# Seven products of quadrant sums for 14 of 22 feed-forward tiles, the last product in thirds, and the gate from one table

## The chip, the core and the metric

One core of a Trainium2 chip runs the whole program. The metric is the device time of one execution in microseconds (us), lower being better. Three runs of the kernel before took 2994.84, 2996.77 and 2997.41 us; the median is 2996.77.

## The reference, cut to what matters

The model is a chain of ten stages on 512 tokens of 1024 features in float32: two hybrid attention layers, then twice (feed-forward, HGRN2 and pooling mixer, memory cross-attention, feed-forward), and a last norm. The change lives in the four feed-forward stages (D_FF = 2816):

```python
def swiglu(h, w1, w3, w2):
    return (jax.nn.silu(h @ w1) * (h @ w3)) @ w2

x = x + 0.5 * swiglu(rmsnorm(x, ffn1_norm[l]), ffn1_w1[l], ffn1_w3[l], ffn1_w2[l])
```

## The kernel before, in words

Activations stand feature-major: features on the 128 partitions, the 512 tokens along the free axis, so x is eight tiles x0 to x7 of 128x512. Every dense product runs on the tensor engine (PE) in three passes: an operand is split exactly into a leading part (hi) and the rest (lo), and `mm3` (lines 296 to 298) issues hi*hi, hi*lo and lo*hi for each block of 128 features:

```python
self.nc.tensor.matmul(ps, ah, bh, start=first and i == 0, stop=False)   # L296
self.nc.tensor.matmul(ps, ah, bl, start=False, stop=False)              # L297
self.nc.tensor.matmul(ps, al, bh, start=False, stop=last and i == n - 1)  # L298
```

Each matmul has its own weight load (LDWEIGHTS, shown as PEld). Weights come from HBM through the SP queue in pieces `wraw` of up to 128x1024 (L270, four buffers); `chunk` (L287, L288) lets the scalar engine (ACT) write `whi` by a copy that rounds and the vector engine (DVE) write `wlo` by a subtraction. `whi` and `wlo` have two buffers each, so that the next chunk of weights is prepared while the present one is used.

A feed-forward stage (`ffn`) goes in two halves of 11 tiles. A tile is 128 columns of w1 and the same 128 columns of w3, each a unit of eight blocks, 24 matmuls of 512 columns, into one PSUM bank `mm` of three. The evacuation `ev` runs two units later. After the w1 unit, DVE multiplies the bank by `rt`, the tokens' 1/rms (L886, into `si`); silu is made of an exponential, a logarithm and an exponential on ACT (L504 to L506) between a clamp (L501) and two multiplications (L888, L889) on POOL (GpSimd). After the w3 unit DVE multiplies the bank by the gate (L893), ACT rounds the result into `hh` and DVE subtracts for `hl` (L256, L257). The w2 product of the half follows: eight units of 11 blocks (33 matmuls), each added to its x tile by one DVE operation (L901). So a stage has 22 x 48 + 8 x 66 = 1584 matmuls of 512 columns. In the second half the x tiles are at once split for the next stage (`ready`, L262, L263).

The order of the work on each engine is set by the order in which the program issues it, by the delays of `later` and `tick` (steps run so many units later), and by the tile framework's scheduler, which may move ready instructions ahead. On the chip each engine then runs its own list in order.

Of the kernel before, what the change touches and what calls it, by code (L numbers as in the profile page):

```python
# [29 lines left out]
NH = DFF // P // 2  # L30
# [6 lines left out]
# tiles of a tag get their room in program order, so work that runs at its own pace has a tag of its own  # L37
SLOTS = {"slot": 34, "alt": 12, "far": 11}
# [10 lines left out]
        "ffn1": "ql sb si",  # L49
        "mix": "hO ha1 ham hd he hk msh qh ql",  # L50
        "xa": "ql xq",
        "ffn2": "ql sb si",
# [3 lines left out]
# engines of the steps that more than one can take: V(ector), P(ool), A(ctivation)  # L56
# [42 lines left out]
def _const_layout():  # L99
    c = Cols()  # L100
    for name, w in (("ones", 128), ("eps", 1), ("bd", 128), ("ident", 128), ("dil", 512),
                    ("causal", 512), ("tri", 512), ("reset", 512), ("diag", 32), ("pool", 64)):
        c.add(name, w)
    return c
# [3 lines left out]
CONST_EARLY = CONST.at["dil"][0]  # L108


def _constants():
# [21 lines left out]
    # pairs s, t of 32 tokens in the two halves of a segment of 2 hs tokens  # L133
# [11 lines left out]
def _pack(i):  # L145
# [5 lines left out]
    # 8 frequencies x 16 blocks of 32 tokens  # L151
# [37 lines left out]
    for n in ("ffn1", "ffn2"):  # L189
        w1, w3, w2 = f(f"{n}_w1_2"), f(f"{n}_w3_2"), f(f"{n}_w2_2")  # L190
        A[f"{n}_w13"] = per(lambda l: np.concatenate([_chunks(w1[l], 128), _chunks(w3[l], 128)], 3))
        half = NH * P
        A[f"{n}_w2"] = per(lambda l: np.stack([_chunks(w2[l][h * half:(h + 1) * half], 128) for h in range(2)]))
# [13 lines left out]
# ---------------------------------------------------------------- the program  # L207
class Prog:
# [9 lines left out]
    # tiles  # L218
# [26 lines left out]
    def cst(self, name):  # L245
        o, w = CONST.at[name]
        return self.c[:, o:o + w]
# [5 lines left out]
    # exact split of float32 into two float32r parts  # L253
# [12 lines left out]
    def raw(self, flat, pieces=1):  # L266
# [4 lines left out]
        return t  # L271

    def chunk(self, ap, kt, c):
        """One chunk of a weight: both parts, [128, kt, c]."""
        nc = self.nc
        early, self.early = self.early, None
        hi = self._new(self.sb, [P, 2080], R, "whi", 2, "whi")
        lo = self._new(self.sb, [P, 2080], R, "wlo", 2, "wlo")
        n = kt * c
        flat = ap.rearrange("p k c -> p (k c)")  # L280
        step = -(-kt // 2) * c
        for o in range(0, n, step):
            e = min(o + step, n)
            raw = early[o // step] if early else self.raw(flat[:, o:e])
            for a in range(o, e, step // 2 if early else step):
                b = a + step // 2 if early else e
                nc.scalar.activation(hi[:, a:b], raw[:, a - o:b - o], AF.Copy)  # L287
                nc.vector.tensor_tensor(lo[:, a:b], raw[:, a - o:b - o], hi.bitcast(F32)[:, a:b], op=ALU.subtract)  # L288
        v = lambda t: t[:, :n].rearrange("p (k c) -> p k c", k=kt)
# [1095 lines left out]
```

## Time and profile before

| what | value |
|---|---|
| median of three runs | 2996.77 us |
| profiled execution: span from first to last instruction | 2992.6 us |
| its own time beside the span | not listed apart; the span lies 4.2 us below the runs' median |
| PE busy | 2929.1 us, 98% |
| DVE, ACT, POOL busy | 1674.1, 1406.6, 745.2 us |
| mean granted PE clock | 0.994 |

The span is what the profile divides among engines and lines; what the launch adds lies outside it. PE's busy time counts overlapping matmuls once. A matmul's own duration (0.39 us at 512 columns) is longer than the distance to the next one's start, because matmuls overlap in the pipeline; the distance from start to start is what a matmul costs in a row of them.

### The profile page before, as it was taken

What the parts mean: (1) busy time and instruction counts of PE and PEld (TensorE: products, weight loads), DVE (VectorE), ACT (ScalarE), POOL (GpSimd) and SP (SyncE); (2) the same over time, 40 slices, a digit from 0 to 9 for tenths busy, and PEclk for the clock granted to TensorE, in tenths of its full rate; (3) what the DMA queues carried; (4) which work ended last, traced back from release to release, by engine and by line L of the source; (5) the groups of instructions that cost most, each with busy time, mean ns of one, the idle gap of its engine ahead of it and who ended that gap; (6) DMA issues with size and microseconds to landing.
All of it is one profiled execution on the core that took longest, in us unless ns stands there. A gap on an engine that the chain in (4) does not pass through costs nothing.

```text
span 2992.6 us, 39832 instructions
## 1 busy us (share of the span) xinstructions
PE 2929.1 (98%) x15544; PEld 2372.5 (79%) x15544; DVE 1674.1 (56%) x2698; ACT 1406.6 (47%) x2334; POOL 745.2 (25%) x613
## 2 busy tenths in 40 slices
PE   7999999999999999999999999999999999999997
PEld 6777877778788887798888888888888798888886
DVE  7976678766533337785643333433347976643333
ACT  5876467664532434464443233432434654443342
POOL 3101131011331323331032132321323330132231
PEclk9999999999999999999999999999999999999999
DMA  4432233322223232243132323223232242232322
GB/s 159 121 103 82 95 113 94 106 80 94 96 80 107 87 96 89 68 131 99 57 99 79 111 90 99 97 76 111 83 107 83 79 134 85 71 98 79 110 75 76
DMA packets 93436, 284.10 MB, mean 95 GB/s; under 512 B 12656, under 2 KB 13056, under 8 KB 93120
## 3 DMA queue, kind: packets, MB, share of 16 engines
q1 hardware_dynamic: 92928, 281.26, 29.5%
q8 instruction: 122, 2.00, 0.3%
q14 instruction: 66, 0.54, 0.1%
q10 hardware_dynamic: 288, 0.28, 0.0%
q0 software_dynamic: 32, 0.02, 0.0%
HBM read 261.46 MB, written 2.10 MB: 88 GB/s over the span
## 4 chain that ended last, share of the span: by engine, by line
PE 86%; DVE 7%; ACT 2%; issue 1%; POOL 0%; DMA 0%; DVEq 0%; ACTq 0%; POOLq 0%
PE mm L296 27%; PE mm L297 26%; PE mm L298 26%; PE po L712 2%; DVE wlo L288 1%; PE pt L701 1%; PE aux L687 1%; PE aux L421 1%; PE aux L688 1%; PE po L1103 0%; PE aux L296 0%; PE aux L298 0%; PE aux L297 0%; ACT whi L287 0%; DVE hw L1020 0%
## 5 line engine op out<-in xcount | busy, mean ns | idle before, releaser
L296 PE MATMUL mm<-xsh,whi 128*128 128x512 f32 x2304 | 926.9, 403 | 16.9 <-DVE pol L263 8.1
L297 PE MATMUL mm<-xsl,whi 128*128 128x512 f32 x2304 | 910.5, 395 | 8.0 <-DVE xsl L263 7.6
L298 PE MATMUL mm<-xsh,wlo 128*128 128x512 f32 x2304 | 911.2, 396 | 0.0
L287 ACT ACTIVATE whi<-wraw 128x1024 fp32r<-128x1024 f32 (+4 forms) x526 | 498.5, 984 | 572.2 <-PE mm L297 408.0
L288 DVE TENSOR_TENSOR wlo<-wraw,whi 128x1024 fp32r<-128x1024 f32 (+4 forms) x526 | 596.5, 1165 | 110.4 <-ACT whi L287 106.2
L296 PEld LDWEIGHTS mm<-xsh,whi 128*128 128x128 f32 x2304 | 435.6, 189 | 128.4 <-issue 13.1
L297 PEld LDWEIGHTS mm<-xsl,whi 128*128 128x128 f32 x2304 | 435.7, 189 | 108.2 <-DVE xsl L263 14.5
L298 PEld LDWEIGHTS mm<-xsh,wlo 128*128 128x128 f32 x2304 | 435.1, 189 | 101.4 <-DVE wlo L288 0.2
L501 POOL TENSOR_SCALAR sb<-si 128x512 f32<-128x512 f32 x88 | 130.8, 1487 | 770.0 <-DVE si L886 770.0
L433 POOL TENSOR_TENSOR sq<-sq,sq 128x512 f32<-128x512 f32 (+1 forms) x97 | 132.0, 1361 | 722.5 <-ACT sq L430 711.0
L893 DVE TENSOR_TENSOR sb<-mm,sb 128x512 f32<-128x512 f32 x88 | 60.9, 692 | 435.2 <-POOL sb L889 435.2
L297 PE MATMUL mm<-hl,whi 128*128 128x512 f32 x704 | 277.4, 394 | 0.0
L296 PE MATMUL mm<-hh,whi 128*128 128x512 f32 x704 | 277.2, 394 | 0.0
L298 PE MATMUL mm<-hh,wlo 128*128 128x512 f32 x704 | 276.7, 393 | 0.0
L504 ACT ACTIVATE sb<-sb 128x512 f32<-128x512 f32 x88 | 55.8, 634 | 464.1 <-POOL sb L501 464.1
L901 DVE SCALAR_TENSOR_TENSOR x<-mm,x 128x512 f32<-128x512 f32 x64 | 44.3, 692 | 306.7 <-PE mm L298 306.7
L297 PEld LDWEIGHTS mm<-hl,whi 128*128 128x128 f32 x704 | 132.3, 188 | 30.8
L296 PEld LDWEIGHTS mm<-hh,whi 128*128 128x128 f32 x704 | 131.8, 187 | 31.3
L298 PEld LDWEIGHTS mm<-hh,wlo 128*128 128x128 f32 x704 | 132.5, 188 | 30.3
L886 DVE TENSOR_TENSOR si<-mm,rt 128x512 f32<-128x512 f32 x88 | 60.9, 692 | 134.4 <-PE mm L298 134.2
L889 POOL TENSOR_TENSOR sb<-sb,si 128x512 f32<-128x512 f32 x88 | 113.9, 1296 | 67.3 <-ACT sb L506 67.3
L888 POOL TENSOR_TENSOR si<-si,rt 128x512 f32<-128x512 f32 x88 | 114.9, 1306 | 7.3
(360 smaller groups left out, 4580.8 us busy)
## 6 DMA issues: line engine op xcount, KB each, us to landing
wraw<-in_ffn_w_dram SPq DMA_DIRECT2D x176, 512.0 KB
wraw<-in_ffn_w_dram SPq DMA_DIRECT2D x64, 384.0 KB
wraw<-in_ffn_w_dram SPq DMA_DIRECT2D x64, 320.0 KB
z<-z SPq DMA_DIRECT2D x128, 128.0 KB
wraw<-in_w_out_dram SPq DMA_DIRECT2D x32, 512.0 KB
wraw<-in_w_qk_dram SPq DMA_DIRECT2D x30, 512.0 KB
wraw<-in_w_g_dram SPq DMA_DIRECT2D x16, 512.0 KB
wraw<-in_w_gate_dram SPq DMA_DIRECT2D x16, 512.0 KB
```

Of the source, the lines that this page charges most:

```text
L287: nc.scalar.activation(hi[:, a:b], raw[:, a - o:b - o], AF.Copy)
L288: nc.vector.tensor_tensor(lo[:, a:b], raw[:, a - o:b - o], hi.bitcast(F32)[:, a:b], op=ALU.subtract)
L296: self.nc.tensor.matmul(ps, ah, bh, start=first and i == 0, stop=False)
L297: self.nc.tensor.matmul(ps, ah, bl, start=False, stop=False)
L298: self.nc.tensor.matmul(ps, al, bh, start=False, stop=last and i == n - 1)
L433: (eng or self.on("acc")).tensor_tensor(acc[:, :n], acc[:, :n], sq[:, :n], op=ALU.add)
L501: clamp.tensor_scalar(t, x, -40.0, None, op0=ALU.max)
L712: nc.tensor.matmul(self.po[rows, j * P:], v[j][:, 64 * h:64 * h + 64], ptS[b][:, o:o + T - j * P], start=j == 0, stop=j == 2)
L886: nc.vector.tensor_tensor(s, ps, r["r"], op=ALU.mult)
L888: nc.gpsimd.tensor_tensor(s, s, r["r"], op=ALU.mult)
L889: nc.gpsimd.tensor_tensor(b, b, s, op=ALU.mult)
L893: nc.vector.tensor_tensor(b, ps, b, op=ALU.mult)
```

## The change

In each feed-forward stage, 14 of the 22 tiles are computed another way. Take for one tile the matrix A of two rows (128 columns of w1; the same of w3) by two columns (the even-numbered 128-feature blocks of x; the odd-numbered), and B of two rows (even and odd blocks of x) by two columns (tokens 0 to 255, tokens 256 to 511). A B has four quadrants. Instead of eight quadrant products, seven products of sums of quadrants are made (Winograd's form of Strassen's method), each over four feature blocks and 256 tokens: 12 matmuls of 256 columns, 84 in all for the tile instead of 48 of 512 columns. The sums of the weights' quadrants (`sums`, L962) are made on DVE for each tile and then split into hi and lo as the raw weights are; the sums of x's quadrants (`seven_operands`, L906 to L909) are made once for a stage, during the first two tiles. The products' banks are put together by additions on DVE (L962 again, into a tile `early`). `PLAIN` says which tiles remain as they were ("1"), now in the order w1, w3 of `gated_pair`.

```diff
-NH = DFF // P // 2
+THIRDS = (8, 7, 7)
+PLAIN = ("11100100", "0010010", "0010010")
...
-        A[f"{n}_w13"] = per(lambda l: np.concatenate([_chunks(w1[l], 128), _chunks(w3[l], 128)], 3))
+        A[f"{n}_w13"] = per(lambda l: np.stack([_chunks(w[l], 128)[:, :, o::2] for w, o in ((w1, 0), (w1, 1), (w3, 1), (w3, 0))], 2))
...
+    def half(self, n):
+        return [self._new(self.sb, [P, 1040], R, "w", 8, "w" + e)[:, :n] for e in "hl"]
...
+    def seven(self, flat, mv, r, done):
...
+        def p0():
+            st["e"], st["o"] = (self.raw(flat[:, o:o + 1024]) for o in (0, 1024))
+            st["a"] = self.half(1024)
+            self.parted(st["a"], st["e"])
+        def p1():
+            f, e, o = wide("sums", 2), st["e"], st["o"]
+            st["f"] = f
+            add(f[:, :512], o[:, 512:], o[:, :512])
+            add(f[:, 512:], f[:, :512], e[:, :512])
+            st["s"] = self.half(1024)
+            self.parted(st["s"], f)
+        def p2():
+            g, e, o = wide("sums", 2), st["e"], st["o"]
+            add(g[:, :512], e[:, :512], o[:, 512:])
+            add(g[:, 512:], st["f"][:, 512:], e[:, 512:])
+            st["t"] = self.half(1024)
+            self.parted(st["t"], g)
+        def p3():
+            st["d"] = self.half(512)
+            self.parted(st["d"], st["o"][:, :512])
...
+        def m4():
+            product("y2", 1, "d", 0, "t4")
+            q, g = st["q"], self.s(nm="sb")
+            self.later(2, lambda: add(q[:, H:3 * H], st["y2"], st["v"]))
+            self.later(3, lambda: nc.gpsimd.tensor_tensor(g, q[:, :T], r["r"], op=ALU.mult))
+            self.later(4, lambda: nc.scalar.activation(g, g, AF.Silu))
+            self.later(5, lambda: nc.vector.scalar_tensor_tensor(g, q[:, T:], -1.0, g, op0=ALU.mult, op1=ALU.mult))
+            self.later(6, lambda: done(g))
+        return [p0, p1, p2, p3], [m1, m2, m6, m5, m7, m3, m4]
...
+    def run_pairs(self, units, after):
+        for f in units[0][0]:
+            f()
+        for i, (_, steps) in enumerate(units):
+            more = list(units[i + 1][0] if i + 1 < len(units) else [after])
+            for n, f in enumerate(steps):
+                f()
+                self.tick()
+                if n >= 2 and n % 2 == 0 and more:
+                    more.pop(0)()
+            for f in more:
+                f()
...
+            def done(j, b, added):
+                hh, hl = self.s(R, "hh"), self.s(R, "hl")
+                nc.scalar.activation(hh, b, AF.Copy)
+                if added:
+                    nc.scalar.activation(hl, b, AF.Copy, scale=-1.0)
+                    nc.gpsimd.dma_start(out=hl, in_=b, accum_op=ALU.add)
                 else:
-                    hid[j] = self.split(b, nm="h")
+                    nc.vector.tensor_tensor(hl, b, hh.bitcast(F32), op=ALU.subtract)
...
             def ev2(m, ps):
-                nc.vector.scalar_tensor_tensor(self.x[m], ps, 0.5, self.x[m], op0=ALU.mult, op1=ALU.add)
+                t = self.s(nm="xr")
+                nc.vector.scalar_tensor_tensor(t, ps, 0.5, r["r"], op0=ALU.mult, op1=ALU.mult)
+                nc.vector.tensor_tensor(self.x[m], t, self.x[m], op=ALU.add)
```

The remaining parts of the change:

- The w2 product goes in thirds of 8, 7 and 7 tiles instead of halves of 11: the same 528 matmuls, but 24 units instead of 16, each evacuated by two DVE operations (L1101, L1102) instead of one. The factor 1/rms of the w3 side is applied there.
- The gate is one ACT activation with the function Silu (L941, L1039). The clamp and two of POOL's three operations of a tile are gone; in a seven-product tile POOL multiplies by 1/rms (L1038). ACT loads Silu's table at the start of each stage and the old one back before the third w2 product: eight table loads more.
- In ten seven-product tiles of a stage, `hl` comes from an ACT copy of the negative of `hh`'s source and an adding DMA from the POOL queue (L1075, L1076), the rest from a DVE subtraction (L1078).
- Weight buffers are now eight tiles of 128x1040 (`half`; four pairs `wh`, `wl`), used by all dense products; a chunk of eight blocks by 256 columns takes two pairs, each freed by itself. The masks, rotary tables and `part` share buffers (tag `early`) with the feed-forward's sums.

How the order moves, first on PE, at the second group of tiles of the first feed-forward stage. Before (`mm` is a bank, `xsh`, `xsl` are x's parts, 512 columns), where a w3 unit ends and a w1 unit begins:

```order
L297 MATMUL mm_2047_8168<-xsl_2011_7955,whi_2033_8084 128x512
L298 MATMUL mm_2047_8168<-xsh_2010_7954,wlo_2034_8085 128x512
L296 MATMUL mm_2050_8202<-xsh_1976_7753,whi_2043_8158 128x512
L297 MATMUL mm_2050_8202<-xsl_1977_7754,whi_2043_8158 128x512
L298 MATMUL mm_2050_8202<-xsh_1976_7753,wlo_2044_8159 128x512
```

Now, in a seven-product tile of the second third, where product m2 (weights `wh_2323`, the even and odd columns of w1) ends and m6 (weights `wh_2326`, sums) begins in the other half of the same bank; `t1h`, `t1l` are sums of x's quadrants:

```order
L313 MATMUL mm_2335_9265<-xsh_2109_8056,wh_2323_9228 128x256
L314 MATMUL mm_2335_9265<-xsl_2110_8057,wh_2323_9228 128x256
L315 MATMUL mm_2335_9265<-xsh_2109_8056,wl_2324_9229 128x256
L313 MATMUL mm_2335_9265<-t1h_2126_8116,wh_2326_9235 128x256
L314 MATMUL mm_2335_9265<-t1l_2127_8117,wh_2326_9235 128x256
L315 MATMUL mm_2335_9265<-t1h_2126_8116,wl_2327_9236 128x256
```

Each matmul has half the columns and still its own weight load; a new pair of weights comes every 12 or 24 matmuls of 256 columns instead of every 48 of 512.

On DVE, one whole tile before (evacuations `si`, `sb`, the next tile's two `wlo`, and `hl`):

```order
L886 TENSOR_TENSOR si_2048_8193<-mm_2040_8128,rt_2027_8039 128x512
L893 TENSOR_TENSOR sb_2049_8194<-mm_2047_8168,sb_2049_8194 128x512
L288 TENSOR_TENSOR wlo_2054_8233<-wraw_2055_8234,whi_2053_8232 128x1024
L288 TENSOR_TENSOR wlo_2054_8233<-wraw_2056_8238,whi_2053_8232 128x1024
L257 TENSOR_TENSOR hl_2052_8229<-sb_2049_8194,hh_2051_8228 128x512
```

Now, the first two seven-product tiles of the second third (`early_2336`, `ab_2342` and `sb_2347` belong to the first, `wl_2340` to `wl_2352` to the second's weights; the second's sums stand a dozen rows earlier, between the w2 evacuations):

```order
L285 TENSOR_TENSOR wl_2340_9297<-wraw_2337_9292,wh_2339_9296 128x1024
L962 TENSOR_TENSOR early_2336_9290<-mm_2335_9265,cd_2334_9263 128x2x256
L285 TENSOR_TENSOR wl_2345_9330<-sums_2343_9326,wh_2344_9329 128x1024
L962 TENSOR_TENSOR ab_2342_9325<-aux_2341_9300,early_2336_9290 128x512
L962 TENSOR_TENSOR early_2336_9290<-aux_2341_9300,ab_2342_9325 128x256
L285 TENSOR_TENSOR wl_2350_9365<-sums_2348_9361,wh_2349_9364 128x1024
L285 TENSOR_TENSOR wl_2352_9369<-wraw_2338_9294,wh_2351_9368 128x512
L962 TENSOR_TENSOR early_2336_9290<-mm_2346_9333,ab_2342_9325 128x512
L1040 SCALAR_TENSOR_TENSOR sb_2347_9360<-early_2336_9290,sb_2347_9360 128x512
```

Where five DVE instructions stood for a tile, these nine stand, and four additions for `sums` beside them.

Third, PE at the end of the second third, where the w2 product begins: `hh_2454` and `hl_2455` are the result of the third's last tile, `mm_2459` is the first w2 unit and `mm_2463` the second:

```order
L315 MATMUL mm_2459_10030<-hh_2449_9971,wl_2447_9955 128x512
L313 MATMUL mm_2459_10030<-hh_2454_10020,wh_2446_9954 128x512
L313 MATMUL mm_2463_10058<-hh_2362_9450,wh_2457_10026 128x512
L314 MATMUL mm_2459_10030<-hl_2455_10021,wh_2446_9954 128x512
L315 MATMUL mm_2459_10030<-hh_2454_10020,wl_2447_9955 128x512
L314 MATMUL mm_2463_10058<-hl_2363_9451,wh_2457_10026 128x512
```

The last tile's result is read by the 19th matmul of the first unit (in the third of eight tiles by the 22nd, with no matmul of the second unit in between), where before it was read by the 31st.

## Rows read from the trace of the kernel before

**Rows 1.** The page: span, and busy time of each engine.

```profile
span 2992.6 us, 39832 instructions
PE 2929.1 (98%) x15544; PEld 2372.5 (79%) x15544; DVE 1674.1 (56%) x2698; ACT 1406.6 (47%) x2334; POOL 745.2 (25%) x613
```

**Rows 2.** Busy time by windows, over two of the four feed-forward stages.

```profile
core 0: us, PE busy (x) PEld busy (x) DVE busy (x) ACT busy (x) POOL busy (x), PEclk, DMA share, GB/s
765.00:1132.00 367.00, 366.87 (x1584) 297.16 (x1584) 143.24 (x174) 136.10 (x187) 101.51 (x74) 1.00 0.29 94
...
1843.00:2210.00 367.00, 366.97 (x1584) 297.15 (x1584) 140.43 (x169) 133.53 (x184) 100.75 (x73) 1.00 0.29 95
```

**Rows 3.** Timeline of PE (start us, us): first and last of three unbroken 256-column runs.

```profile
419.23 0.28 PE L296 MATMUL mm<-whi,xsh 128*128 128x256 f32 x1
...
424.76 0.28 PE L298 MATMUL mm<-whi,xsl 128*128 128x256 f32 x1
...
47.58 0.28 PE L296 MATMUL mm<-whi,xsh 128*128 128x256 f32 x1
...
52.92 0.28 PE L298 MATMUL mm<-whi,xsl 128*128 128x256 f32 x1
...
1291.52 0.28 PE L297 MATMUL mm<-msl,whi 128*128 128x256 f32 x1
...
1301.28 0.28 PE L298 MATMUL mm<-msh,wlo 128*128 128x256 f32 x1
```

**Rows 4.** Groups by line and shape, whole span (busy us, mean ns | idle before): weight loads.

```profile
L298 PEld LDWEIGHTS mm<-whi,msl 128*128 128x128 f32 x128 | 24.2, 189 | 0.0
```

**Rows 5.** Groups by line and shape, DVE, within a feed-forward stage (790 to 1100 us).

```profile
L288 DVE TENSOR_TENSOR wlo<-wraw,whi 128x1024 fp32r<-128x1024 f32 x36 | 42.4, 1221 | 0.3 <-ACT whi L287 0.3
L257 DVE TENSOR_TENSOR hl<-sb,hh 128x512 fp32r<-128x512 f32 x21 | 14.4, 686 | 0.0
L893 DVE TENSOR_TENSOR sb<-mm,sb 128x512 f32<-128x512 f32 x20 | 13.8, 692 | 102.7 <-POOL sb L889 102.7
...
L263 DVE SCALAR_TENSOR_TENSOR xsl<-x,prm,xsh 128x512 fp32r<-128x512 f32 x3 | 2.2, 746 | 0.0
```

**Rows 6.** The same, whole span: a DVE operation of 256 columns from a bank.

```profile
L1237 DVE TENSOR_TENSOR xk<-mm,rt 128x256 f32<-128x256 f32 x16 | 6.6, 414 | 1.3 <-PE mm L298 1.2
```

**Rows 7.** The same, ACT, 790 to 1100 us; the table load from the start.

```profile
L287 ACT ACTIVATE whi<-wraw 128x1024 fp32r<-128x1024 f32 x36 | 36.2, 1053 | 26.4 <-PE mm L297 26.4
...
L506 ACT ACTIVATE sb<-sb 128x512 f32<-128x512 f32 x20 | 12.6, 632 | 0.6
L256 ACT ACTIVATE hh<-sb 128x512 fp32r<-128x512 f32 x20 | 12.3, 616 | 0.2 <-DVE sb L893 0.2
...
L532 ACT ACT_TABLE_LOAD x1 | 1.3, 1283 | 1.2 <-PEq L1374 1.2
```

**Rows 8.** The same, POOL, 790 to 1100 us.

```profile
L888 POOL TENSOR_TENSOR si<-si,rt 128x512 f32<-128x512 f32 x20 | 26.1, 1306 | 1.7
```

**Rows 9.** Timeline, end of the first stage's second half of tiles, start of its w2 product.

```profile
1061.55 0.69 DVE L886 TENSOR_TENSOR si<-mm,rt 128x512 f32<-128x512 f32 x1 [2.37 <-PE mm L298]
...
1062.33 1.49 POOL L501 TENSOR_SCALAR sb<-si 128x512 f32<-128x512 f32 x1 [6.08 <-DVE si L886]
...
1063.85 0.64 ACT L504 ACTIVATE sb<-sb 128x512 f32<-128x512 f32 x1 [6.14 <-POOL sb L501]
...
1066.71 0.39 PE L298 MATMUL mm<-xsh,wlo 128*128 128x512 f32 x1
...
1067.37 0.69 DVE L893 TENSOR_TENSOR sb<-mm,sb 128x512 f32<-128x512 f32 x1 [5.13 <-POOL sb L889]
...
1068.29 0.62 ACT L256 ACTIVATE hh<-sb 128x512 fp32r<-128x512 f32 x1
```

**Rows 10.** Busy time by windows, in the first mixer stage.

```profile
1263.00:1268.00 5.00, 5.00 (x13) 3.84 (x13) 4.59 (x9) 4.21 (x10) 0.73 (x1) 0.50 0.01 3
```

**Rows 11.** The page: the DMA queue that POOL's own transfers use.

```profile
q0 software_dynamic: 32, 0.02, 0.0%
```

More of the change, by code (lines that the diff above doesn't have):

```diff
@@ L36 @@
 TWO_PI = 2.0 * math.pi
-SLOTS = {"slot": 34, "alt": 12, "far": 11}
+SLOTS = {"slot": 34, "alt": 12, "far": 11, "early": 4}
 TAGS = {
@@ L190, in _pack @@
         w1, w3, w2 = f(f"{n}_w1_2"), f(f"{n}_w3_2"), f(f"{n}_w2_2")
-        A[f"{n}_w13"] = per(lambda l: np.concatenate([_chunks(w1[l], 128), _chunks(w3[l], 128)], 3))
-        half = NH * P
-        A[f"{n}_w2"] = per(lambda l: np.stack([_chunks(w2[l][h * half:(h + 1) * half], 128) for h in range(2)]))
+        A[f"{n}_w13"] = per(lambda l: np.stack([_chunks(w[l], 128)[:, :, o::2] for w, o in ((w1, 0), (w1, 1), (w3, 1), (w3, 0))], 2))
+        A[f"{n}_w2"] = per(lambda l: _chunks(w2[l], 128))
     w2i = f("w_in_2")
@@ L324, in part @@
             ps = held["ps"]
-            self.mm3(ps[:, :n], [pair(*held["w"], i) for i in range(k, e)], k == 0, e == kt)
+            self.mm3(ps[:, :n], [pair(held["w"], i) for i in range(k, e)], k == 0, e == kt)
             if e == kt:
@@ L340, in dense @@
                 cs = slice(j * P, (j + 1) * P)
[L341 removed]
+                pair = lambda w, k, cs=cs: (self.at(w, k, cs), (act[k][0][:, :n], act[k][1][:, :n]))
                 i = ci * (c // P) + j
@@ L520, in setup @@
         self.pr = self.keep([P, PARAM.n], F32, "prm")
-        self.c = self.keep([P, CONST.n], F32, "cst")
+        self.c = self.keep([P, CONST_KEPT], F32, "cst")
+        wide = lambda nm: self._new(self.sb, [P, 2 * T], F32, "early", SLOTS["early"], nm)
+        m, k, rope, part = (wide(n) for n in ("mask", "tri", "rope", "part"))
+        self.masks = {"dil": m[:, :T], "causal": m[:, T:], "tri": k[:, :T]}
+        self.selb = k[:96, T:].bitcast(BF).rearrange("p (h t) -> p h t", t=P)
+        self.C, self.S = rope[:, :T], rope[:, T:]
+        self.part = [part[:, :T], part[:, T:]]
         self.lev = self.keep([P, 5, 32], U8, "lev")
-        self.selb = self.keep([96, 8, P], BF, "selb")
         self.x = [self.keep([P, T], F32, f"x{k}") for k in range(KD)]
-        self.C, self.S = self.keep([P, T], F32, "ropeC"), self.keep([P, T], F32, "ropeS")
         self.cT = self.keep([96, T], BF, "cT")
-        self.part = [self.keep([P, T], F32, f"part{i}") for i in range(2)]
         self.npart = 0
@@ new lines, in gated_pair, with load, part, one @@
+    def gated_pair(self, flat, xs, r, done):
+        st = {}
+        tiles = []
+        def load(half):
+            raw = self.raw(flat[:, 1024 * half:1024 * half + 1024])
+            w = self.half(1024)
+            self.parted(w, raw)
+            tiles.append(w)
+        def part(which, q):
+            if q == 0:
+                st["ps"] = self.ps("mm")
+            ps = st["ps"]
+            blocks = range(2 * q, 2 * q + 2)
+            k = lambda i: 2 * (i % 4) + (i // 4 + which) % 2
+            self.mm3(ps, [(tuple(t[:, i * P:i * P + P] for t in tiles[which]), xs[k(i)]) for i in blocks], q == 0, q == 3)
+            if q == 3:
+                self.later(4, (lambda: one(ps)) if which == 0 else (lambda: three(ps)))
+        def one(ps):
+            b = st["b"] = self.s(nm="sb")
+            self.nc.vector.tensor_tensor(b, ps, r["r"], op=ALU.mult)
+            self.later(1, lambda: self.nc.scalar.activation(b, b, AF.Silu))
+        def three(ps):
+            b = st["b"]
+            self.nc.vector.tensor_tensor(b, ps, b, op=ALU.mult)
+            self.later(1, lambda: done(b))
+        parts = [lambda w=w, q=q: part(w, q) for w in range(2) for q in range(4)]
+        return [lambda: load(0), lambda: load(1)], parts
```

169 lines of the change are left out of this document (121 added, 48 removed).

## The prediction

> **What bounds the kernel now.** I read the page first, then the busy time by windows, then the timeline of PE, then the groups by shape. The page shows PE busy for 2929.1 of 2992.6 us [rows 1], and the reader should see that no other engine is above 56%. That is an average over ten stages, so the windows come next: over two of the four feed-forward stages PE is busy for 366.87 and 366.97 of 367.00 us, at a granted clock of 1.00, with exactly the 1584 matmuls that the code counts for a stage [rows 2]. PE never waits there; DVE works 39% of the time, ACT 37%, POOL 28%. So a feed-forward stage costs 367.00 / 1584 = 0.2317 us per matmul of 512 columns, and only fewer or cheaper matmuls shorten it. What ACT and POOL do for the gate is hidden: Silu's table, by itself, gains nothing.
>
> **What a half-wide matmul costs.** The trace has matmuls of 256 columns, in other stages, each with its own weight load as the change has them. Three unbroken runs of them [rows 3]: 48 matmuls from 419.23 to 424.76 us, 5.53 / 47 = 0.1177 us from start to start; 48 from 47.58 to 52.92, 0.1136; 83 from 1291.52 to 1301.28, 0.1190. I take 0.1177, a run inside dense products as in the stage at issue, and keep the others as bounds. A weight load lasts 0.189 us [rows 4], longer than that distance, and yet the runs keep it: loads go on while earlier matmuls run. The Trainium skill ("TensorE: Matmul & The Clock Gate", Part 3, on what overlaps) says otherwise, that a load overlaps a matmul in flight only when it goes to another group of rows; these loads fill the whole array, so by that rule the change would pay for 36 more loads a tile, 36 x 0.189 = 6.8 us at the row's duration, against some 1.2 us gained. The runs contradict it, and the sum goes by the runs.
>
> **The sum, part by part.**
>
> A tile left as it is costs PE 48 x 0.2317 = 11.12 us. A seven-product tile costs 84 x 0.1177 = 9.89 us, so 1.23 us less; with 14 tiles in four stages, 56 x 1.235 = **69.1 us less**. With 0.1136 it is 88, with 0.1190 it is 63. The w2 product keeps its 528 matmuls and its cost.
>
> DVE must cover its new work. A seven-product tile has three `wl` of 1024 columns (3 x 1.22), one of 512 (0.69), four sums (4 x 0.69), three additions of 512 columns from banks (3 x 0.69) and one of 256 (0.41), and the gate's last multiplication (0.75) [rows 5, 6]: 10.4 us, and 0.69 for `hl` in four tiles of 14. A plain tile has 2 x 1.22 + 3 x 0.69 = 4.5 us. Two seven-product tiles in a row therefore ask DVE for 20.8 us in PE's 19.8, but every pair is followed by a plain tile or by w2 units, where DVE asks 4.5 of 11.1 us and 1.22 + 2 x 0.69 = 2.6 of 4.9 to 5.6. In a third of five and two it is 61 of 71.7 us. The lag within a pair is covered by the weight buffers: the four pairs are one tile ahead. The first is free when m2 has run, 2.8 us into a tile, and is read again when the tile ends, at 9.9; the refill takes 1.05 us on ACT [rows 7] and 1.22 on DVE; 4.8 us are left, and the other pairs have at least as much. I price this at nothing; without the cover it is the second rival. ACT has 3 x 1.05 + 5 x 0.63 = 6.3 us of the tile's 9.9. POOL falls from three operations a tile to one of 1.31 us [rows 8] and, for ten tiles a stage, an adding DMA. That queue carries almost nothing now [rows 11], so the trace has no price for such a DMA; its `hl` is read by w2 at least one whole tile (9.9 us) later, and I price it at nothing, at most at a few us through that bound.
>
> The sums of x, four sets a stage, are 4 x (4 x 0.41 + 2 x 0.69) = 12.1 us of DVE in the first tiles. With the evacuations of three plain tiles (6.2), weights for two plain (4.9) and the first seven-product tile (7.1) and the 1/rms (2.1), DVE has 32.4 us to do in the 33.4 of three plain tiles. That is tight: 0 to 3 us a stage, I take 0.5, **2 us** in all.
>
> At a third's end PE goes on to w2 and soon needs the last tile, which is a seven-product tile in every third. From its last matmul's start, with durations of [rows 5, 7, 8] and hand-offs read from the timeline [rows 9] (bank to DVE 0.27 after the matmul's end, DVE to POOL 0.09, POOL to ACT 0.03, DVE to ACT 0.23, and 0.1 assumed from ACT to DVE): 0.55, addition to 1.24, POOL to 2.64, Silu to 3.30, multiplication to 4.15, `hh` to 5.0, `hl` to 5.8. The first unit starts 0.12 us in and reads `hh` after 18 matmuls, at 4.29 us, in a third of seven, and `hl` two matmuls later: 0.71 + 0.34 = 1.05 us of waiting. In a third of eight it reads them at 4.99 and 5.23: 0.6. That is 0.6 + 2 x 1.05 = 2.7 a stage, **10.8 us** in all; before, the chain was four steps shorter and its reader the 31st matmul, so nothing was lost. Bounds: 4 us if the hand-offs are shorter, 38 if a weight refill (1.05 + 1.22) stands in front of the chain each of the 12 times.
>
> At a stage's end each x tile takes one more DVE operation, 0.69 us. It is hidden where the next stage reads the last x tile after several units' matmuls; at the program's end, where the final norm waits for it, it is **0.7 us**. The eight table loads, 1.28 us each [rows 7], stand on ACT, which is far from full, and cost nothing; if each stopped the gate chain they would cost under 1.3 x 8 = 10. The finer weight buffers may help the other stages by a few us, and those stages have stretches at the lower clock (0.50, that is 1.2 GHz, in 5 us of the first mixer [rows 10]), which may fall otherwise: together 0, within 5 us either way.
>
> Sum: 69.1 - 10.8 - 2 - 0.7 = 55.6 us less than the profiled span of 2992.6, which is 2937.0. The profile lists no time of its own beside the span; the runs' median is 4.2 above it, so I predict **2941 us**.
>
> **The rivals.**
>
> (A) The forecast, 0.80. PE stays the bound, the range of this case alone is 2925 to 2955: the low end has shorter matmuls than 0.1177 and few waits, the high end 14 us more of waits.
>
> (B) Slower: DVE sets the pace of pairs of seven-product tiles, 0.04. DVE runs its list in order, and a `wl` can't start before ACT has written its `wh`. If DVE stood idle for ACT's 1.05 us at all four refills, a tile would take it 14.6 us; a pair falls behind by 9.5, the buffers cover 4.8, and PE loses 4.7 for each of the 24 pairs (six a stage): 113 us, so 3054. It decides from 13.4 us a tile on, where the loss of 2.3 a pair eats the 55.6. Against it: in the order of DVE the sums of the tile after and the evacuations stand between the refills, and ACT is only 63% full.
>
> (C) Slower: weight loads set the pace, 0.01. If a matmul could not start sooner than 0.189 us after the one before, a tile would take 84 x 0.189 = 15.9 us, 4.8 more than plain: +267, 3264. The runs of [rows 3] speak against it.
>
> (D) Faster by less: small waits in the tiles, 0.14. Seven products need four fresh pairs of weights and four banks where two units needed two of each. If PE loses 0.2 to 0.7 us a tile, or the thirds' ends cost their upper bound, 11 to 39 us go: 2952 to 2980.
>
> (E) No change, 0.01: waits that just balance the gain.
>
> **How the numbers follow.** A measurement of this kernel can tell about 0.2%, 6 us. (A) and (D) are faster by more: 0.94; (E) 0.01; (B) and (C) 0.05. The time is (A)'s. The range goes from 2925 to 2970, which holds (A) but for its tails and the larger part of (D).
>
> **What would show it.** In the profile after, a feed-forward stage should last about 353 us with PE over 98% busy and 1584 - 14 x 48 + 14 x 84 = 2088 matmuls; runs of 256 columns at 0.117 to 0.119 us; DVE busy for 260 to 270 us of the stage; PE's waits on `hh` and `hl` about 2.7 us a stage; the other stages as long as before. It would be wrong if PE waits on `wl` (then B), if 256-column matmuls follow each other at over 0.125 us (then C or a new limit), or if the waits at the thirds' ends are over 1.5 us each (then D).

## The result, and the profile after

The changed kernel takes 2955.51 us (median of four runs, 2952.66 to 2957.7) where the kernel before took 2996.18 beside it: a ratio of 0.9864, with a 95% interval of 0.985 to 0.9878. That is 40.7 us less; the forecast was 55.6 less and 2941 us, with 2925 to 2970 as its range. The page's first lines and one of its DMA rows:

```profile
span 2953.7 us, 44940 instructions
...
PE 2871.5 (97%) x17560; PEld 2425.6 (82%) x17560; DVE 2089.3 (71%) x3354; ACT 1487.6 (50%) x2406; POOL 539.1 (18%) x445
...
q0 software_dynamic: 5792, 10.50, 2.0%
```

Beside [rows 1], PE lost a point of its share although its work shrank: the span fell by 38.9 us, PE's busy time by 57.6. So something like 19 us that PE did not wait for before it waits for now. The windows over one feed-forward stage show the same beside [rows 2]:

```profile
core 0: us, PE busy (x) PEld busy (x) DVE busy (x) ACT busy (x) POOL busy (x), PEclk, DMA share, GB/s
1850.36:2205.77 355.41, 351.44 (x2092) 309.62 (x2091) 245.93 (x328) 151.02 (x199) 46.78 (x31) 1.00 0.36 106
```

The forecast said 353 us, 2088 matmuls (four of other work lie in the window) and DVE busy for 260 to 270; it is 355.4. DVE's busy time is 246, because the window counts successive operations that overlap once; their durations add up to 261, as forecast. PE stands still for 4.0 us of the stage. The waits of PE over the whole span (engine, line and tile waited for; us, times, longest) name the place:

```profile
PE mm L313 <- ACT hh L1073: 15.1, 12, 1.3
...
PE mm L314 <- DVE hl L1078: 0.9, 4, 0.2
```

Twelve waits on `hh`, one at the end of each third. Now the stages, from start to start of PE's matmuls: the border into a feed-forward stage is the 528th weight matmul ahead of the first that reads `hh` in the first half or third (in both kernels that many make 11 plain tiles, or eight tiles of a first third), its end the last matmul that reads `hh`. The last column is an experiment further down.

| stretch, us | before | after | after, sums on DVE (`e9`) |
|---|---|---|---|
| start to the first feed-forward stage | 757.9 | 760.4 | 755.1 |
| first feed-forward stage | 369.9 | 362.2 | 356.3 |
| first mixer and cross-attention | 376.3 | 372.3 | 370.0 |
| second feed-forward stage | 367.2 | 355.4 | 355.5 |
| third | 367.6 | 355.2 | 355.3 |
| second mixer and cross-attention | 369.3 | 374.8 | 369.6 |
| fourth feed-forward stage | 366.9 | 355.3 | 355.3 |
| rest to the span's end | 17.4 | 18.0 | 17.9 |

Three of four feed-forward stages gain 11.6 to 12.4 us, the first only 7.7, and of the other stages one is 4.0 shorter and one 5.5 longer. Two questions follow: what the 14 tiles really gain, and where the rest of it goes.

The first is answered by one tile. Its first matmul, its last, and the next tile's first:

```profile
898.04 0.28 PE L313 MATMUL pt<-xsh,wh 128*128 128x256 f32 x1
...
907.83 0.28 PE L315 MATMUL mm<-t2h,wl 128*128 128x256 f32 x1
907.94 0.28 PE L313 MATMUL pt<-xsh,wh 128*128 128x256 f32 x1
```

84 matmuls in 9.90 us. The other tiles agree: in all eight later thirds the seven tiles take 71.55 to 71.59 us, two plain tiles 2 x 48 x 0.2313 = 22.2 of it, which leaves 49.4 / 420 = 0.1175 us for a matmul of 256 columns (0.2313 is what 512 columns cost in the halves before, 122.12 / 528). So a seven-product tile costs 9.87 us, a plain one 11.10.

The second, at the end of a third. This is the timeline (start and duration in us) of the second third of the first stage; its last product is read from bank `mm`, and the chain to `hh` goes through DVE, POOL, ACT, DVE, ACT:

```profile
969.30 1.09 DVE L285 TENSOR_TENSOR wl<-wraw,wh 128x896 fp32r<-128x896 f32 x1 [0.67 <-ACT wh L284]
...
969.48 0.28 PE L315 MATMUL mm<-t2h,wl 128*128 128x256 f32 x1
...
970.31 0.68 DVE L962 TENSOR_TENSOR early<-mm,ab 128x512 f32<-128x512 f32 x1
...
970.91 1.08 DVE L285 TENSOR_TENSOR wl<-wraw,wh 128x896 fp32r<-128x896 f32 x1
...
971.08 2.06 POOL L1038 TENSOR_TENSOR sb<-early,rt 128x512 f32<-128x512 f32 x1 [12.96 <-DVE early L962]
...
973.18 0.63 ACT L1039 ACTIVATE sb<-sb 128x512 f32<-128x512 f32 x1 [2.55 <-POOL sb L1038]
...
973.84 0.69 DVE L1040 SCALAR_TENSOR_TENSOR sb<-early,sb 128x512 f32<-128x512 f32 x1 [1.85 <-ACT sb L1039]
974.57 0.63 ACT L1073 ACTIVATE hh<-sb 128x512 fp32r<-128x512 f32 x1 [0.76 <-DVE sb L1040]
...
975.25 0.73 PE L313 MATMUL mm<-hh,wh 128*128 128x512 f32 x2 [1.34 <-ACT hh L1073]
```

PE starts on `hh` 5.77 us after the start of the tile's last matmul, where the sum had 5.0. Two links are longer than assumed: the addition starts 0.83 behind that matmul, not 0.55, because DVE is busy with a weight's `wl` until then, and POOL takes 2.06 us, not the 1.31 of [rows 8]. In the thirds of eight tiles it is 1.17 and 2.11 to 2.14 us, and PE starts on `hh` 6.25 us behind. The w2 product of a third of seven lasts 40.8 us from its first matmul to the next work's, 168 x 0.2316 = 38.9 without waits, that of eight 46.4 instead of 44.5: 1.9 us at each end, 22.9 in all twelve.

Why POOL takes longer is in the rows as well. First a multiplication with nothing beside it, then one in which DVE works on two tiles that both lie in SBUF:

```profile
941.13 1.28 POOL L1038 TENSOR_TENSOR sb<-early,rt 128x512 f32<-128x512 f32 x1 [13.80 <-DVE early L962]
...
951.40 1.21 DVE L285 TENSOR_TENSOR wl<-sums,wh 128x1024 fp32r<-128x1024 f32 x1
951.58 2.79 POOL L1038 TENSOR_TENSOR sb<-early,rt 128x512 f32<-128x512 f32 x1 [5.34 <-DVE early L962]
952.53 0.68 DVE L962 TENSOR_TENSOR sums<-sums,wraw 128x512 f32<-128x512 f32 x1
```

The same instruction takes 1.28 and 2.79 us. Fitted over the 56 of them, POOL's time is 1.28 us plus 0.88 us for each us in which such a DVE operation runs (none beside 24 of them, 0.9 to 1.0 us beside 12, 1.7 beside 20), and that leaves 8 ns unexplained. In all 32 of the longer ones DVE had started before POOL, and it kept its usual time. Beside a DVE operation that reads a PSUM bank POOL loses nothing: another operation of POOL's (L432) took 1.29 us with 1.25 us of that beside it. Before, none of the operations of [rows 8] happened to have DVE beside it. The Trainium skill ("SBUF — State Buffer", section "Who interferes with whom") states it: a DVE instruction with two SBUF inputs contends with a GpSimd instruction that reads SBUF; one with at most one does not, as long as it is outside the modes that use both of DVE's ports. The trace agrees, with 2.79 us beside two SBUF inputs and 1.29 beside a bank; the prediction did not look for it.

### The profile page after: what moved, and what is told of

It reads as the page before. It is cut to its first block, busy times and chain, and to the rows that moved or that the text cites. A ratio compares the mean times of both kernels' runs of the same rounds, so it can differ in the third digit from the quotient of the medians.

```text
span 2953.7 us, 44940 instructions
## 1 busy us (share of the span) xinstructions
PE 2871.5 (97%) x17560; PEld 2425.6 (82%) x17560; DVE 2089.3 (71%) x3354; ACT 1487.6 (50%) x2406; POOL 539.1 (18%) x445
## 5 line engine op out<-in xcount | busy, mean ns | idle before, releaser
L284 ACT ACTIVATE wh<-wraw 128x1024 fp32r<-128x1024 f32 (+3 forms) x494 | 489.2, 991 | 488.8 <-PE mm L314 357.9
L313 PE MATMUL mm<-xsh,wh 128*128 128x512 f32 (+1 forms) x1856 | 699.5, 377 | 18.2 <-ACT xsh L267 11.6
L285 DVE TENSOR_TENSOR wl<-wraw,wh 128x1024 fp32r<-128x1024 f32 (+3 forms) x494 | 572.6, 1160 | 176.8 <-ACT wh L284 171.6
L314 PE MATMUL mm<-xsl,wh 128*128 128x512 f32 (+1 forms) x1856 | 685.0, 369 | 6.1 <-DVE xsl L268 6.1
L315 PE MATMUL mm<-xsh,wl 128*128 128x512 f32 (+1 forms) x1856 | 683.6, 369 | 0.0
L313 PEld LDWEIGHTS mm<-xsh,wh 128*128 128x128 f32 x1856 | 352.2, 190 | 91.1 <-ACT xsh L267 13.3
L314 PEld LDWEIGHTS mm<-xsl,wh 128*128 128x128 f32 x1856 | 352.4, 190 | 63.4 <-DVE xsl L268 8.6
L315 PEld LDWEIGHTS mm<-xsh,wl 128*128 128x128 f32 x1856 | 352.2, 190 | 62.0 <-DVE wl L285 0.3
L313 PE MATMUL mm<-hh,wh 128*128 128x512 f32 x704 | 277.9, 397 | 15.1 <-ACT hh L1073 15.1
L1038 POOL TENSOR_TENSOR sb<-early,rt 128x512 f32<-128x512 f32 x56 | 111.8, 1996 | 988.3 <-DVE early L962 938.8
L314 PE MATMUL mm<-hl,wh 128*128 128x512 f32 x704 | 278.8, 396 | 0.9 <-DVE hl L1078 0.9
L1101 DVE SCALAR_TENSOR_TENSOR xr<-mm,rt 128x512 f32<-128x512 f32 x96 | 66.4, 692 | 164.1 <-PE mm L315 164.0
L267 ACT ACTIVATE xsh<-x,prm 128x512 fp32r<-128x512 f32 x96 | 68.8, 718 | 118.3 <-DVE x L849 35.2
```

Of the source, the lines that this page charges most:

```text
L267: self.nc.scalar.activation(hi[:, :n], src, AF.Copy, scale=g)
L284: self.nc.scalar.activation(hi, src, AF.Copy)
L285: self.nc.vector.tensor_tensor(lo, src, hi.bitcast(F32), op=ALU.subtract)
L1038: self.later(3, lambda: nc.gpsimd.tensor_tensor(g, q[:, :T], r["r"], op=ALU.mult))
L1101: nc.vector.scalar_tensor_tensor(t, ps, 0.5, r["r"], op0=ALU.mult, op1=ALU.mult)
```

## The experiments

Two theories stood for the missing gain. The first, "chain": the seven products gain what was forecast, and PE pays at the thirds' ends for a long chain behind the last tile. Other matmuls that PE can run meanwhile are called cover below. The second: something else is late there (weights, DVE's list), or the other parts of the change cost by themselves. Ratios below are against the kernel before, with 95% intervals; the reference point is the changed kernel, 2955.5.

**e1_two_units.** The first two w2 units take turns.

```diff
-            self.go(last)
+            for u in last[:2]:
+                u.prep()
+            for u in last[:2]:
+                for f in u.parts[:3]:
+                    f()
+            for u in last[:2]:
+                for f in u.parts[3:]:
+                    f()
+                self.tick()
+            self.go(last[2:])
```

> The first two w2 units of a third run interleaved: six blocks of each (36 matmuls of 512 columns, 8.3 us) before either reads the last tile's hh. Theory 'chain' (PE waits 1.86 us at each of the 12 thirds' ends because hh of the last tile comes 5.8 to 6.2 us after the tile's last matmul and PE has only 18 or 21 matmuls to do before): no wait is left, 12 x 1.86 = 22 us less than the changed kernel's 2955.5, that is 2933 (2930 to 2938). Rival 'weights': what is late at the start of w2 is the preparing of its weights on ACT and DVE, which the second unit now needs 4.2 us earlier; PE then waits on wh or wl instead of hh, and the time stays at 2950 to 2957.

Measured: 2935.46 us, ratio 0.9797 [0.9783, 0.9812]. The group of matmuls that read `hh` has no idle time ahead of it any more (last number; 15.1 in the changed kernel):

```profile
L313 PE MATMUL mm<-hh,wh 128*128 128x512 f32 x704 | 278.0, 395 | 0.0
```

The w2 products last 38.97 and 44.53 us, the bare cost of their matmuls. It follows that the weights were in time and the chain alone was late.

**e2_dve_mult_last.** A shorter chain instead of more cover.

```diff
-            self.later(3, lambda: nc.gpsimd.tensor_tensor(g, q[:, :T], r["r"], op=ALU.mult))
+            self.later(3, lambda: (nc.vector if last else nc.gpsimd).tensor_tensor(g, q[:, :T], r["r"], op=ALU.mult))
...
-                    units.append(self.seven(flat, mv, r, lambda b, j=j: done(j, b, j < nh - 2)))
+                    units.append(self.seven(flat, mv, r, lambda b, j=j: done(j, b, j < nh - 2), j == nh - 1))
```

> In the last tile of each third the multiplication by 1/rms is made by DVE instead of POOL. Theory 'chain': the POOL step takes 2.06 us there (1.29 us where DVE does nothing beside it) and two hand-offs; on DVE it takes 0.69 us right behind the addition, so hh comes 1.45 us earlier and of the 1.86 us of waiting about 0.4 is left: 12 x 1.45 = 17 us less, 2938 (2936 to 2944). Rival 'DVE order': the wl of a w2 unit (1.09 us) stands between addition and multiplication in DVE's list, and only 0.4 us of each wait goes: 2950 (2947 to 2956).

Measured: 2937.12 us, ratio 0.9805 [0.9791, 0.982]. The loss at the thirds' ends falls from 1.9 us to 0.2 (seven tiles) and 0.4 to 0.5 (eight). The number is that of the theory, but the way isn't. DVE at the end of the second third:

```profile
969.14 0.68 DVE L962 TENSOR_TENSOR early<-mm,ab 128x512 f32<-128x512 f32 x1
969.74 1.08 DVE L285 TENSOR_TENSOR wl<-wraw,wh 128x896 fp32r<-128x896 f32 x1
970.74 0.69 DVE L1038 TENSOR_TENSOR sb<-early,rt 128x512 f32<-128x512 f32 x1
...
972.12 0.69 DVE L1040 SCALAR_TENSOR_TENSOR sb<-early,sb 128x512 f32<-128x512 f32 x1 [0.70 <-ACT sb L1039]
```

A `wl` does stand between addition and multiplication, as the rival had it, and `hh` is ready 5.18 us after the start of the tile's last matmul instead of 5.72: only 0.54 us are won. The larger part is that the order which the scheduler makes now has PE read the last `hh` as the 23rd matmul of the w2 product instead of the 19th, behind four of the second unit, 4 x 0.23 = 0.93 us. So this run speaks for cover, as `e1` does; what POOL's step alone was worth it doesn't tell.

**e3_all_plain.** All tiles plain; the sums of x are made and not used.

```diff
-PLAIN = ("11100100", "0010010", "0010010")
+PLAIN = ("11111111", "1111111", "1111111")
```

> All 22 tiles of a stage plain; thirds, Silu's table, the finer weight buffers and the sums of x (now unused) stay. Theory 'seven products gain 1.234 us a tile, thirds cost by the long chain alone': 56 x 1.234 = 69 us more and 12 x 1.86 = 22 less, because a plain last tile has a chain without POOL and the additions: 3002 (2998 to 3007), a feed-forward stage 367 us, no wait on hh. Rival 'other parts cost': the thirds, Silu or the buffers take time by themselves, and the kernel stays some 10 us or more above that: 3010 to 3025.

Measured: 3002.53 us, ratio 1.0021 [1.0012, 1.0031]. The difference to the changed kernel is 47.0 us. The w2 products here carry only 0.6 us beyond their matmuls, 22.3 less than in the changed kernel, and 47.0 + 22.3 = 69.3, where the 56 tiles were to gain 69.1. Without seven products the second stage lasts 366.8 us, about as before (367.2), so thirds, Silu's table and table loads cost and gain nothing there. But the whole is 6.8 us slower than before, and that lies outside the three undisturbed feed-forward stages: this kernel's first one takes 373.9 us, its second mixer stretch 375.9.

**e4_nineteen.** Five more tiles of a stage by seven products: does DVE keep up?

```diff
-PLAIN = ("11100100", "0010010", "0010010")
+PLAIN = ("11100000", "0000000", "0000000")
```

> 19 of 22 tiles by seven products (only the first three plain). Theory 'PE is the bound, DVE's lag is covered by the weight buffers': 20 more tiles x 1.234 = 25 us less, 2931 (2927 to 2938), waits at the thirds' ends as before. Rival (B of the prediction) 'DVE sets the pace in runs of seven-product tiles': DVE has 10.4 us and more to do in 9.87; if the waits for ACT add to it (14.6 us a tile), up to 4.7 us a tile are lost and the time goes over 3000; by its bare busy time, 0.6 us a tile, 2931 to 2943 with PE waiting on wl.

Measured: 2975.82 us, ratio 0.9934 [0.9918, 0.9951]: 20 us slower than with 14 tiles. Neither forecast was right. PE never waits inside the tiles: seven of them in a row take 68.8 to 69.2 us, 7 x 9.87 = 69.1. But DVE falls behind all the same, and the end of the third shows it. PE and DVE, end of the second third:

```profile
966.66 0.28 PE L315 MATMUL mm<-t2h,wl 128*128 128x256 f32 x1
...
970.76 0.68 DVE L962 TENSOR_TENSOR early<-mm,ab 128x512 f32<-128x512 f32 x1
...
975.66 1.22 PE L313 MATMUL mm<-hh,wh 128*128 128x512 f32 x2 [4.55 <-ACT hh L1073]
976.68 0.63 PE L314 MATMUL mm<-hl,wh 128*128 128x512 f32 x1
977.11 0.63 PE L315 MATMUL mm<-hh,wl 128*128 128x512 f32 x1
```

The addition behind the last matmul starts 4.1 us after it instead of 0.83 (at the other ends 2.3 to 4.2). All that the buffers let DVE put off is due here, and the waits on `hh` grow from 15.1 to 42.1 us. And the wait costs more than itself: the matmuls behind it are 0.43 us apart instead of 0.23. The windows show the granted clock:

```profile
976.00:980.00 4.00, 4.00 (x10) 3.09 (x10) 2.56 (x4) 0.95 (x1) 0.00 (x0) 0.50 0.00 2
```

0.50, that is 1.2 GHz, behind a standstill of 4.55 us. In all, the w2 products carry 69 us beyond their matmuls instead of 22.9: 46 lost, 25 gained.

**e8_pool_twice.** Is such a loss one for one? The chain is made longer.

```diff
+            if last:
+                self.later(3, lambda: nc.gpsimd.tensor_tensor(g, q[:, :T], r["r"], op=ALU.mult))
             self.later(4, lambda: nc.scalar.activation(g, g, AF.Silu))
```

> In the last tile of each third POOL makes the same multiplication twice, which lengthens the chain by 1.3 to 2.1 us. Theory 'the chain sets the wait, one for one': 12 x 1.3 to 2.1 = 15 to 25 us more, 2971 to 2981, each third's end 3.1 to 3.9 us of waiting. Theory 'a longer wait costs more than itself': as after the waits of 3.5 to 4.7 us in the kernel with 19 tiles, the granted clock falls to 0.50 behind the wait, for 3.4 to 6.8 us, and each third's end loses another 1.5 to 3.5 us: 2990 to 3020.

Measured: 2982.81 us, ratio 0.9951 [0.9936, 0.9966]: 27.3 us more, between the two forecasts. The waits on `hh` are 29.5 us, 14.4 more, about 1.2 each, for a second multiplication of 1.28 us. The third's end that was shown above, the wait and then the stretch behind it:

```profile
978.20:980.80 2.60, 0.41 (x2) 0.00 (x0) 0.69 (x1) 1.03 (x2) 0.78 (x1) 1.00 0.44 159
981.80:985.20 3.40, 3.40 (x10) 2.71 (x9) 2.13 (x3) 0.95 (x1) 0.00 (x0) 0.50 0.03 7
```

Ten of the 12 ends have such a stretch of 3.4 us at 0.50; the changed kernel, which waits 1.1 to 1.3 us at a time there, has it at none. The two ends without it give its price: the w2 product lasts 41.75 us at one of them and 43.0 to 43.3 at the other ends of seven tiles, 47.5 and 48.8 to 49.1 in the thirds of eight, so 1.2 to 1.6 us for the clock. Without it the product is only 0.9 to 1.1 us longer than in the changed kernel, somewhat less than the wait grew; in the thirds of eight the 0.23 us that PE waited for `hl` right behind `hh` are now inside the wait. In all the w2 products carry 49.1 us beyond their matmuls, 26.2 more than in the changed kernel. The chain sets the wait nearly one for one, and at ten ends the clock adds more than the longer wait does.

**e5_nineteen_cover.** `e4`'s tiles with the edits of `e1` and `e2` (no new lines).

> 19 of 22 tiles by seven products, the first two w2 units interleaved, and the last tile's multiplication on DVE. Theory 'DVE falls behind in runs of seven-product tiles and PE pays for it only at the third's end': with 19 tiles hh came up to 9 us after the last tile; the cover grows from 4.2 or 4.9 us to 8.3 and the chain loses 1.4, so nearly all of the 69 us that e4 lost at the 12 thirds' ends go: 2935 less 20 x 1.234, that is 2911 (2908 to 2918). Rival 'the lag moves on': DVE's own w2 work (wl and evacuations) stands behind the late tile, PE waits on wl or on a bank instead, and it stays at 2920 to 2945.

Measured: 2906.11 us, ratio 0.9695 [0.968, 0.9709], 5 us better than forecast. The w2 products take 38.97 to 39.14 and 44.43 to 44.55 us. With enough other work between, DVE's lag costs nothing: the four feed-forward stages together are 24.3 us shorter than in `e1`, for 20 more tiles at 1.235. The rest of the 29 us by which it is faster than `e1` lies in other stages.

**e6_block_order.** For the first feed-forward stage, whose first third takes 91.2 us where the other three take 84.3.

```diff
-            blocks = range(2 * q, 2 * q + 2)
+            blocks = [4 * (n % 2) + n // 2 for n in (2 * q, 2 * q + 1)]
...
-            self.mm3(ps, [(tuple(t[:, i * P:i * P + P] for t in tiles[which]), xs[k(i)]) for i in blocks], q == 0, q == 3)
+            self.mm3(ps, [(tuple(t[:, i * P:i * P + P] for t in tiles[which]), xs[k(i)]) for i in (blocks if not which else blocks[::-1])], q == 0, q == 3)
```

> Plain tiles take the blocks of x in the order 0 to 7 instead of the even ones first. Theory 'block order': in the first feed-forward stage PE reaches x6 as the fourth block, while x becomes final tile by tile, which makes the start lose 6.9 us instead of 3.0: 3 to 4 us less, 2952, with the first stage's tiles 3 to 4 us shorter and nothing else moved. Rival 'x is late as a whole': the last x tile itself becomes ready 4.4 us later than before, whatever the order: the wait only moves to x7 and the time stays at 2955.

Measured: 2956.01 us, ratio 0.9858 [0.9844, 0.9873]: no change, and the first third still takes 91.2 us. The theory of the block order falls; x is late as a whole.

**e7_no_adding_dma.** `hl` always by DVE.

```diff
-                    units.append(self.seven(flat, mv, r, lambda b, j=j: done(j, b, j < nh - 2)))
+                    units.append(self.seven(flat, mv, r, lambda b, j=j: done(j, b, False)))
```

> hl by a DVE subtraction in all seven-product tiles, no ACT copy of the negative and no adding DMA. DVE gets 40 x 0.69 = 27.5 us more. Theory of the prediction (that DMA costs nothing, DVE's lag is covered): same time, 2955 (2951 to 2959). Rival 'DVE lag': 0.69 us more a tile leave DVE later at the third's end, as in the kernel with 19 tiles; each of the 12 waits grows by 0.7 to 2 us: 2964 to 2980.

Measured: 2955.43 us, ratio 0.9856 [0.984, 0.9873]. The adding DMAs cost nothing, as priced, and gain nothing either at 14 tiles.

**e9_sums_on_dve.** What makes x late ahead of the first feed-forward stage? In the changed kernel two clamps of the gate there (DVE L518, 0.42 us where POOL does nothing beside them) end only 0.3 us behind POOL's addition of squares, which had started first:

```profile
753.20 2.07 POOL L450 TENSOR_TENSOR sq<-sq,sq 128x512 f32<-128x512 f32 x1 [1.36 <-ACT sq L447]
754.04 1.51 DVE L518 TENSOR_SCALAR gt<-gt 128x512 f32<-128x512 f32 x1
...
759.90 1.61 POOL L450 TENSOR_TENSOR sq<-sq,sq 128x512 f32<-128x512 f32 x1 [4.63 <-ACT sq L447]
760.27 1.52 DVE L518 TENSOR_SCALAR gt<-gt 128x512 f32<-128x512 f32 x1
```

```diff
-          "pts0": "A", "pts1": "A", "pts2": "A", "att": "A", "gg": "V", "acc": "P", "clamp": "V", "place": "P", "sl":
+          "pts0": "A", "pts1": "A", "pts2": "A", "att": "A", "gg": "V", "acc": "V", "clamp": "V", "place": "P", "sl":
```

> The changed kernel with the running sums of x's squares (97 additions of two tiles in SBUF) on DVE instead of POOL. Theory 'blocked ends of stages': in the changed kernel DVE's clamps (0.42 us alone) take up to 1.5 us while POOL adds squares, eleven of them where the kernel before has four, two of these right ahead of the first feed-forward stage, whose start loses 6.9 us instead of 3.0; without POOL's additions the start loses 3 us again and the hybrid layers gain some: 3 to 6 us less, 2950. Rival 'order of the chains': the last x tiles are late because of the order of their steps on ACT and DVE, not of blocked ports; 67 us more of DVE work can only lengthen it: 2955 to 2965.

Measured: 2937.36 us, ratio 0.9805 [0.9791, 0.9818]: 18 us less, far more than forecast. The last of these clamps here:

```profile
750.90 0.42 DVE L518 TENSOR_SCALAR gt<-gt 128x512 f32<-128x512 f32 x1
```

The table above shows where the time comes from: 5.3 us ahead of the first feed-forward stage, 5.9 in it (its first third takes 85.3 us, 91.2 before the edit), 2.3 and 5.2 in the two mixer stretches; the rest is unchanged.

DVE took over 97 additions, 62.7 us (83 of 512 columns, 14 of 256), and yet the durations of all its operations add up to only 37.4 us more: those that it had before became 25.3 us shorter. Its busy time, which counts overlaps once, rose by 28.9, from 2089.3 to 2118.2. The stretches at a granted clock of 0.50 ahead of the program's end fell with the waits, from 30.7 us in all to 17.1 (20.5 in the kernel before). An addition of 512 columns itself takes 0.69 us on DVE and took 1.54 on average on POOL; how much of the 18 us comes from that and how much from DVE operations that are no longer held up, the run does not tell apart.

**e11_before_sums_dve.** The same word changed in the kernel before.

> The kernel before with the running sums of squares on DVE instead of POOL. Theory 'the change brought the collisions' (in the changed kernel this edit gave 18 us, in the hybrid layers 5.4, at the first feed-forward start 5.9, in the mixers and cross-attentions 2.6 and 5.4): before, the same stages were shorter by about the same amounts already, so little is left to gain: 2990 to 2996. Rival 'the collisions were always there': before, POOL's additions stand in the same chains, and the edit gains as much as in the changed kernel: 2976 to 2982; then the edit explains nothing of the difference between the two kernels.

Measured: 2991.89 us, ratio 0.9985 [0.9976, 0.9994], 2 to 7 us less. So the greater part of `e9`'s 18 us is a loss that the change brought. It isn't told apart stage by stage: in this kernel the first stretch is 3.7 us shorter, the first feed-forward stage 2.2, the mixer stretches 4.7 shorter and 7.6 longer, since the edit moves the order of the work as well.

**e10_nineteen_sums_dve.** The edit of `e9` in `e5`.

> The same edit on the kernel with 19 tiles and interleaved w2 units (2906). Theory 'blocked ends of stages': 3 to 6 us less, 2901 to 2903. Rival 'DVE is too full': the sums of the next stage's norm stand in the last third's w2 product and in its start, no gain or 0 to 10 us more.

Measured: 2888.88 us, ratio 0.9647 [0.9634, 0.966], 17 us less, 107 less than the kernel before. The second feed-forward stage in this kernel, PE without a pause:

```profile
1466.37:1810.44 344.07, 344.07 (x2271) 314.37 (x2270) 282.76 (x389) 163.08 (x223) 50.36 (x29) 1.00 0.37 112
```

**e12_all_mult_dve.** In `e10`, POOL's multiplication on DVE in every seven-product tile.

```diff
-                    units.append(self.seven(flat, mv, r, lambda b, j=j: done(j, b, j < nh - 2), j == nh - 1))
+                    units.append(self.seven(flat, mv, r, lambda b, j=j: done(j, b, j < nh - 2), True))
```

> The fastest kernel so far (19 tiles, interleaved w2 units, sums on DVE; 2888.9) with the multiplication by 1/rms on DVE in all seven-product tiles, not only in the last. Theory 'DVE's lag is paid at the third's end beyond the cover of 8.3 us': DVE gets 0.69 us more for each of 64 tiles, 4 us a third, hh comes 2 to 4 us later and the cover is just used up: 2889 to 2905, with waits on hh again. Rival 'DVE loses more by POOL's port than by the work': without POOL's multiplications DVE's two-input operations never wait for POOL, and the lag stays: 2887 to 2890, no waits on hh.

Measured: 2889.04 us, ratio 0.9642 [0.9629, 0.9655], the same time as `e10`, and no wait on `hh`: 64 x 0.69 us more on DVE did not lengthen the lag beyond the cover.

## Why the prediction was right in kind and 15 us short

- **PE is the bound, and a half-wide matmul costs 0.1177 us.** Right: 0.1175, a tile 9.87 instead of 9.89 us, and 56 x (11.10 - 9.87) = 69 us, the term as forecast; `e3` gives 47.0 + 22.3. The weight loads (0.190 us each) did not set the pace, and rival C falls. The Trainium skill ("TensorE: Matmul & The Clock Gate", Part 3) lists a load as overlapping only when it goes to another group of rows, by which these would not overlap; the same part also names a background weight buffer, by which they may. The trace contradicts the list here as in [rows 3].
- **DVE's work is covered.** Right for this change: no wait on `wl` in the feed-forward tiles, and 261 us of DVE's operations in a stage, where 260 to 270 were forecast. The reason given held for pairs alone. Beyond pairs the lag does not show as PE waiting on `wl` (rival B), but at the third's end, on `hh` (`e4`).
- **Waits at the thirds' ends, 10.8 us.** The step that failed: 22.9 us. It took POOL's operation from [rows 8], where DVE never ran beside it, and DVE as free when the bank was; the rows after have 2.06 us for 1.31, and a `wl` of up to 1.2 us ahead of the addition. In a third of eight both together made 1.9 us of the forecast 0.6. The place and the mechanism were right, as `e1` (more cover, no wait) and `e8` (a longer chain, a longer wait) show; the split between POOL and `wl` is read in the rows and was not tried by itself. 12.1 of the missing 15 to 17 us are here. An end loses 1.9 us, over the 1.5 that the prediction named as the sign of rival D (chance 0.14), and this is D's second form, with the size between the forecast and its bound of 38; the time, 2955.5, lies at the upper edge of A's range and inside D's.
- **Starts, 2 us.** Three stages lose nothing (84.3 us for 8 tiles; 4 x 11.10 + 4 x 9.87 = 83.9, and two matmuls of the norm), so the sums of x are hidden. The first loses 6.9 us where the kernel before lost 3.0, for a reason that the prediction didn't have: x comes late, and behind PE's waits for it the granted clock is 0.50 for 3.4 us, which the kernel before doesn't show there. With the 0.7 us that the third stage's start no longer loses, 3.2 net.
- **Other stages, 0 within 5 us, and 0.7 at the end.** 2.5 - 4.0 + 5.5 + 0.6 = 4.6 us more. The prediction gave these 5 us either way for the lower clock, and the clock is a part of it: over the whole program the stretches at 0.50 are 30.7 us with PE busy for 27.3 of them, before 20.5 with 18.3, by stages 3.4 us more ahead of the first feed-forward stage, 3.4 more in it, 3.4 less in the first mixer stretch and 6.8 more in the second, each in the direction of that stretch's difference. At half speed that is an estimated 4.5 of the 7.8 us of this point and the one before. What sets the waits ahead of such stretches is told by an experiment: `e9` shows that the losses here and at the first stage's start go back when POOL no longer adds squares. That the clamps were blocked is read in the rows; that the new order of work brought more of it follows from `e11` against `e9`, for the sum, not for each stage.
- **Silu, tables, adding DMAs at nothing.** Right (`e3`, `e7`).

Together: 69.1 - 22.9 - 3.2 - 4.6 = 38.4 of the 38.9 us by which the span fell.

## What to carry to other kernels

When PE is the bound, the gain of cheaper products is easy to forecast from a run of such matmuls; what remains is the chain behind the last of them, and it should be given other matmuls for cover before a link of it is made faster. Take an engine's duration for such a chain from rows in which the other engines do what they will do there: here POOL's operation cost 1.28 or 2.79 us, by what DVE did beside it. An engine that falls behind inside a loop need not show there; look for it where its last result is read.

## What the runs showed of the hardware that was not expected

- POOL and DVE hold each other up, and the later one loses: in the 32 multiplications of POOL that DVE's operations of two SBUF inputs preceded, POOL lost 0.88 us for each us of overlap and DVE nothing; where POOL's addition came first, a DVE clamp, which has only one SBUF input, took 1.5 instead of 0.42 us. Moving 63 us of additions from POOL to DVE, the fuller engine, gained 18 us.
- Behind PE's waits of 2.4 to 2.5 us at the thirds' ends (`e8`) the granted clock fell to 0.50 for 3.4 us at ten of 12 places, behind waits of 2.2 to 4.7 us (`e4`) at 11 of 12, behind 1.1 to 1.3 us (the changed kernel) at none.
- What an engine puts off in a loop can be paid in one place: DVE was 3.3 us later at the end of the second third in `e4` than with 14 tiles, while PE had not waited for it in seven tiles in a row.
